# A hybrid decoder layer in float32: the 256 columns of the gate and up products walked in seven other orders

## The chip, the core and the metric

The kernel runs on one core of one Trainium2 chip, the other cores idle. The metric is device time in microseconds of one execution. It was timed twice: 2033.79 and 2034.99 us, median 2034.39. One more execution was taken by the hardware profiler; all lines of "the profile" and "the trace" come from it.

## The reference, cut to what matters

One decoder layer on 512 tokens plus 16 learned meta tokens, width 2048, all in float32:

```python
n = rmsnorm(h, g_mix);  q, k, v, gb, gc, u = split(n @ w_in)
o_attn = stick_breaking_attention(rmsnorm(q), rmsnorm(k), v)      # 8 heads x 128
o_conv = gb * causal_dwconv3(gc * u)                              # 1024 channels
h = h + concat(rmsnorm(o_attn), rmsnorm(o_conv)) @ w_out
n2 = rmsnorm(h, g_ffn)
h = h + (silu(n2 @ w_gate) * (n2 @ w_up)) @ w_down                # 2048 -> 5632 -> 2048
return h[:, 16:]
```

The change is in `n2 @ w_gate` and `n2 @ w_up`.

## The kernel before, in words

Everything is held transposed: channels on the 128 partitions, tokens along the row. Each float32 operand is split into a high part `hi` of TensorE's one-pass format (float32r, four bytes a value) and the rest `lo`, and a product is three products: hi by hi, hi by lo, lo by hi. Weights are the stationary operand in tiles of 128x128 (128 partitions, 128 columns), activations the moving rows, and the sums stand in PSUM.

The gate and up projections are done in **pairs**: for each of the 44 blocks f of 128 channels of the feed-forward, the gate tile and the up tile together form a 2x2 block product over two halves of the input channels and two halves of the tokens. It is done with 7 block products in place of 8, Strassen's way in Winograd's form: sums and differences of blocks go in, and sums of the products come out. `pair_product` (line 756) issues the seven in the order of the blocks 0, 1, 2, 3, 4, 5, 6 (block 5 first in a pair marked `first`) into three PSUM banks named x, z and y, and has ScalarE and VectorE copy or combine a bank behind each product. `block_product` (line 740) is one of the seven: it takes the next split weight block from `next_w` (hi and lo, 8 tiles each) and issues 3 x 8 = 24 matmuls of 256 columns (half of the 512 tokens) on line 754, all into the same 256 columns of one bank. A pair is 7 x 24 = 168 matmuls.

The same two functions also do the convolution's projections before (three times three pairs of 260 columns, moving rows from the tiles nh, nl and blk) and the down projection behind (moving rows from the tiles first and ring; in its first four pairs each bank holds two products side by side, m = 2). In the gate and up stage the moving rows lie in seven tiles f0 to f6. `slots` lays each out as [128 partitions, 2 parts, 8, 256], contiguous, with its data from the fifth element of the tile on; `act_of` hands out one row of 256 columns.

What else goes on during a pair: SyncE's queue loads the next weight quarters (line 172, 512 KB each) into w_buf, VectorE forms their sums (lines 207 and 225), ScalarE and VectorE split them into s_buf (lines 188 and 189), up to three blocks ahead of their use; `gate` (line 1062) forms silu(gate) * up out of gu, VectorE's lines 1064 and 1068 among it, and `store_acts` sends the blocks of the down projection to DRAM over GpSimd's queue (line 1056). The entries of the plan `ents` name the pair that each weight block belongs to; `used[0]` counts the blocks used so far; `conv_pairs` is the number of pairs of the convolution, so that pair number i - conv_pairs is the block f of the feed-forward.

Two other stages that the text speaks of: lines 286 to 290 (`product_steps`) do the input projection, 264 or 512 columns a matmul out of nh and nl, and lines 860 to 862 (`wide_product`) the output projection, 512 columns out of oa and oc.

Of the kernel before, what the change touches and what calls it, by code (L numbers as in the profile page):

```python
# [33 lines left out]
def hybrid_layer(ctx: ExitStack, tc: tile.TileContext, xT, w_in, w_out, w_gu, w_down, vecs, out):  # L34
# [10 lines left out]
    ve, sc, gp, pe = nc.vector, nc.scalar, nc.gpsimd, nc.tensor  # L45

    def open_pool(name, bufs=1, **kw):
        return tc.alloc_tile_pool(name=name, bufs=bufs, reuse_waits="tile", **kw)
# [54 lines left out]
    loads, ents, pairs = [], [], []  # L103
# [38 lines left out]
    conv_pairs = len(pairs)  # L142
# [11 lines left out]
    quads, sums, split_w, used, loaded = {}, {}, [], [0], [0]  # L154
# [25 lines left out]
    def ahead(e):  # L180
        return 3 if e > sixth + 2 else 2
# [27 lines left out]
    def prepare():  # L209
        i, s = ents[len(split_w)]  # L210
        with tc.high_priority():
            if i == "raw":
                split_quad(quads[i, s][0], loads[s][1])
                done_with((i, s))
                return
            n, first = pairs[i]
            second = i == conv_pairs + 1
            b = {q: quads[i, q][0] for q in ("11", "12", "21", "22") if (i, q) in quads}

            def add_t3():  # L220
                add_quads(i, "t3", b["12"], b["22"], second)
                done_with((i, "12"))

            def add_last():
                ve.tensor_tensor(sums["t2"], sums["t2"], b["21"], ALU.add)  # L225
                done_with((i, "21"))

            if s == 0:
                split_quad(b["11"], n, second)
                add_quads(i, "t1", b["11"], b["12"], second)  # L230
                done_with((i, "11"))
            elif s == 1:
                split_quad(sums["t1"], n, second)
                add_quads(i, "t2", sums["t1"], b["22"], second)
                if not first and not second:
                    add_t3()
            elif s == 2:
                split_quad(sums["t2"], n, second)
                if first or second:
                    add_t3()  # L240
            elif s == 3:
                split_quad(b["22"], n)
                done_with((i, "22"))
            elif s == 4:
                split_quad(sums["t3"], n)
            elif s == 5:
                split_quad(b["21"], n)
                if not first:
                    add_last()
            else:  # L250
                if first:
                    add_last()
                split_quad(sums["t2"], n, i == conv_pairs)
# [3 lines left out]
    def next_w():  # L257
        i = used[0]
        used[0] += 1
        while len(split_w) < limit[0] and len(split_w) <= i + ahead(len(split_w)):  # L260
            prepare()
        return split_w[i]
# [423 lines left out]
    for j in range(CONV_FIRST):  # L686
# [4 lines left out]
        for c in (c1, c2):  # L691
            p = pp.tile([P, 2, 512], F32, tag="pp", name="pcu")
# [47 lines left out]
    def block_product(ps, act, start, m=1):  # L740

        hi, lo, n = next_w()
        w, n = ps.shape[-1] // m, n // m
        for wt, part in ((hi, 0), (hi, 1), (lo, 0)):
            for j in range(m):
                p, skip = ps[:, j * w : (j + 1) * w], m > 1 or not start  # L750
                for k in range(n):
                    kk = slice((j * n + k) * P, (j * n + k + 1) * P)
                    first = start and wt is hi and part == j == k == 0
                    pe.matmul(p, wt[:, kk], act(part, k), start=first, stop=wt is lo and k == n - 1, skip_group_check=skip)  # L754

    def pair_product(acts, c1, c2, sides, m=1, fourth=None, second=None):

# [17 lines left out]
        if first:  # L775
            block_product(y, acts[5], True, m)
        block_product(x, acts[0], True, m)
        with tc.high_priority(1 << 20):
            sc.copy(p1, x)
        block_product(z, acts[1], True, m)  # L780
        with tc.high_priority(1 << 20):
            sc.copy(p5, z)
# [140 lines left out]
    for i, j in enumerate(OUT_TILES):  # L923
        half, k = divmod(j, 8)
# [186 lines left out]
    first = open_pool("ring_first", side="right")  # L1111
# [147 lines left out]
```

## Time and profile before

| | |
|---|---|
| timed runs | 2033.79 and 2034.99 us, median 2034.39 |
| profiled execution, span from the first to the last instruction | 2030.6 us |
| the median less the span | 3.8 us |
| mean granted TensorE clock | 1.000 |
| TensorE busy | 2024.3 us, 16158 matmuls |
| VectorE, ScalarE, GpSimd busy | 1720.3, 1050.1, 381.1 us |
| matmuls of line 754 out of f | 7392, from 769.1 to 1607.5 us |
| DMA | 361.70 MB, mean 178 GB/s |

The profile gives no time of its own for the profiled execution, only its span; what lies around the span is taken from the median. How to read the lines: engines are PE (TensorE's matmuls), PEld (its weight loads, which overlap), DVE (VectorE), ACT (ScalarE), POOL (GpSimd), SP (SyncE). `L754 PE MATMUL x<-f,s_buf 128*128 128x256 f32` is line 754 of the kernel: a matmul into tile x out of moving rows f and weights s_buf, 128 rows by 128 columns of the array, 256 columns streamed. Numbers of buffers are left out of tile names. In the view of one line of the program the durations are the least, the median and the greatest in ns, and then come the first and the last start in us. In the timeline, like instructions that follow one another are merged: start, length, instruction, count. The modelled end of a matmul lies behind the start of the next, since they are pipelined; the distance of starts is what adds up to time.

### The profile page before, as it was taken

How to read it: one execution, taken by the hardware profiler on the slowest of the kernel's cores; microseconds unless marked ns; L12 is line 12 of the kernel's file. 1: busy time of each engine (PE TensorE's matmuls, PEld its weight loads, DVE VectorE, ACT ScalarE, POOL GpSimd, SP SyncE). 2: the span in 40 equal slices, each digit the busy share in tenths (PEclk: the TensorE clock that was granted, in tenths of full speed). 3: DMA queues.
4: the chain of work that ended last, by engine and by line, in shares of the span. 5: the costliest groups of instructions: out<-in, count | busy, mean ns of one | idle time of the engine just before them, and what ended most of it. 6: DMA issues, size and time to landing. Idle time of an engine off the chain costs nothing.

```text
span 2030.6 us, 39733 instructions
## 1 busy us (share of the span) xinstructions
PE 2024.3 (100%) x16158; PEld 1961.7 (97%) x16158; DVE 1720.3 (85%) x2202; ACT 1050.1 (52%) x1517; POOL 381.1 (19%) x532
## 2 busy tenths in 40 slices
PE   9999999999999999999999999999999999999999
PEld 8999999999998889999999999999999999999999
DVE  8788877588976779989989989989989989888887
ACT  7666666444444435555555555555555544444443
POOL 0111111220015440111110110110110252222111
PEclk9999999999999999999999999999999999999999
DMA  6243344753366557555555555555555999989864
GB/s 232 84 147 117 123 135 137 252 154 106 105 213 183 186 174 238 169 161 172 166 161 152 166 161 152 166 161 153 166 161 152 292 327 287 245 234 271 226 149 89
DMA packets 162279, 361.70 MB, mean 178 GB/s; under 512 B 13616, under 2 KB 74032, under 8 KB 162096
## 3 DMA queue, kind: packets, MB, share of 16 engines
q1 hardware_dynamic: 79744, 229.47, 35.4%
q0 software_dynamic: 82208, 129.65, 24.4%
q8 instruction: 127, 2.08, 0.4%
q14 instruction: 56, 0.46, 0.1%
q10 hardware_dynamic: 144, 0.04, 0.0%
HBM read 278.50 MB, written 80.61 MB: 177 GB/s over the span
## 4 chain that ended last, share of the span: by engine, by line
PE 97%; DVE 1%; ACT 1%; issue 0%; DMA 0%; POOL 0%; SPq 0%; DVEq 0%; ACTq 0%
PE x L754 40%; PE z L754 20%; PE y L754 10%; PE po L860 3%; PE po L861 3%; PE po L862 3%; PE pv L286 1%; PE pv L288 1%; PE pv L290 1%; PE pq L288 1%; PE pq L290 1%; PE pq L286 1%; PE pk L286 1%; PE pk L288 1%; PE pk L290 1%; PE pcu L286 1%
## 5 line engine op out<-in xcount | busy, mean ns | idle before, releaser
L188 ACT CAST s_buf<-w_buf 128x1024 fp32r<-128x1024 f32 (+2 forms) x665 | 659.3, 991 | 747.7 <-PE x L754 370.7
L189 DVE TENSOR_TENSOR s_buf<-w_buf,s_buf 128x1024 fp32r<-128x1024 f32 (+2 forms) x665 | 766.5, 1153 | 121.2 <-ACT s_buf L188 119.1
L754 PE MATMUL x<-f,s_buf 128*128 128x256 f32 x4224 | 500.4, 275 | 0.0
L754 PEld LDWEIGHTS x<-f,s_buf 128*128 128x128 f32 x4224 | 488.8, 188 | 0.2
L207 DVE TENSOR_TENSOR w_buf<-w_buf 128x1024 f32<-128x1024 f32 (+1 forms) x243 | 278.3, 1145 | 18.5 <-DMA w_buf<-w_in 11.8
L754 PE MATMUL z<-f,s_buf 128*128 128x256 f32 x2112 | 253.6, 275 | 0.0
L754 PEld LDWEIGHTS z<-f,s_buf 128*128 128x128 f32 x2112 | 245.9, 188 | 0.0
L1056 POOL DMA_DIRECT2D fd<-s x147 | 103.9, 919 | 701.9 <-DVE s L301 701.1
L754 PE MATMUL x<-ring,s_buf 128*128 128x256 f32 x1824 | 219.2, 275 | 0.0
L754 PEld LDWEIGHTS x<-ring,s_buf 128*128 128x128 f32 x1824 | 212.5, 188 | 0.0
L754 PE MATMUL y<-f,s_buf 128*128 128x256 f32 x1056 | 126.8, 275 | 0.0
L754 PEld LDWEIGHTS y<-f,s_buf 128*128 128x128 f32 x1056 | 123.1, 188 | 0.1
L1129 POOL DMA_DIRECT2D out_T<-d x62 | 60.8, 1012 | 284.5 <-DVE d L1137 231.8
L754 PE MATMUL z<-ring,s_buf 128*128 128x256 f32 x864 | 105.7, 275 | 0.0
L754 PEld LDWEIGHTS z<-ring,s_buf 128*128 128x128 f32 x864 | 101.5, 188 | 0.0
L225 DVE TENSOR_TENSOR w_buf<-w_buf 128x1024 f32<-128x1024 f32 (+1 forms) x81 | 92.2, 1139 | 0.0
L754 PE MATMUL x<-nh,s_buf 128*128 128x260 f32 x432 | 58.9, 282 | 0.0
L790 DVE SCALAR_TENSOR_TENSOR gu<-z,sides 128x256 f32<-128x256 f32 x44 | 18.7, 425 | 42.7 <-PE z L754 40.8
L754 PEld LDWEIGHTS x<-nh,s_buf 128*128 128x128 f32 x432 | 54.5, 188 | 0.1
L754 PE MATMUL z<-blk,s_buf 128*128 128x260 f32 x432 | 54.6, 282 | 0.0
L286 PE MATMUL pk<-nh,s_buf 128*128 128x264 f32 x256 | 52.6, 287 | 0.5 <-ACT nh L358 0.5
L754 PEld LDWEIGHTS z<-blk,s_buf 128*128 128x128 f32 x432 | 52.9, 188 | 0.0
(344 smaller groups left out, 3318.3 us busy)
## 6 DMA issues: line engine op xcount, KB each, us to landing
w_buf<-w_gu SPq DMA_DIRECT2D x176, 512.0 KB, 3.5
w_buf<-w_in SPq DMA_DIRECT2D x92, 512.0 KB, 3.4
fd<-s POOLq DMA_DIRECT2D x147, 256.0 KB, 5.3
w_buf<-w_down SPq DMA_DIRECT2D x96, 384.0 KB, 4.9
ring<-fd POOLq DMA_DIRECT2D x42, 768.0 KB, 9.0
w_buf<-w_out SPq DMA_DIRECT2D x32, 512.0 KB, 3.5
out_T<-d POOLq DMA_DIRECT2D x62, 256.0 KB, 5.6
fc<-st SPq DMA_DIRECT2D x8, 1040.0 KB, 6.3
```

The source lines that it names most:

```text
L188: sc.copy(hi, src)
L189: in_turn(ve.tensor_tensor(lo, src, hi.bitcast(F32), ALU.subtract), turn)
L207: in_turn(ve.tensor_tensor(sums[name], a, b, ALU.add), turn)
L225: ve.tensor_tensor(sums["t2"], sums["t2"], b["21"], ALU.add)
L286: pe.matmul(ps, wh, ah[:, a:b], start=k == 0, stop=False)
L288: pe.matmul(ps, wh, al[:, a:b], start=False, stop=False)
L290: pe.matmul(ps, wl, ah[:, a:b], start=False, stop=k == last)
L754: pe.matmul(p, wt[:, kk], act(part, k), start=first, stop=wt is lo and k == n - 1, skip_group_check=skip)
L860: pe.matmul(ps, hi[:, kk], ah, start=k == order[0], stop=False)
L861: pe.matmul(ps, hi[:, kk], al, start=False, stop=False)
L862: pe.matmul(ps, lo[:, kk], ah, start=False, stop=k == order[-1])
L1056: gp.dma_start(fd[c][s][:, :, k], t[:, :, i])
```

## The change

`block_product` looks up which pair it serves, and in pairs 4 to 31 of the 44 gate and up pairs hands the matmul both its result and its moving row through `walk`. That views the 256 columns as h bands of b runs of e neighbouring columns and goes through them run by run, the first run of each band, then the second of each, and so on. The same order is used on both sides, so each column's sum ends where it did. With (h, e) = (2, 2), for instance, the columns come as 0, 1, 128, 129, 2, 3, 130, 131 and so on; with (2, 64) as 0 to 63, 128 to 191, 64 to 127, 192 to 255. Pairs 0 to 3 and 32 to 43, the convolution and the down projection keep their plain order. Seven groups of four pairs have a walk each: pairs 4 to 7 (2, 2); 8 to 11 (2, 4); 12 to 15 (2, 16); 16 to 19 (2, 64); 20 to 23 (4, 16); 24 to 27 (4, 4); 28 to 31 (8, 16).

```diff
+        i = ents[used[0]][0]
         hi, lo, n = next_w()
         w, n = ps.shape[-1] // m, n // m
         for wt, part in ((hi, 0), (hi, 1), (lo, 0)):
...
-                    pe.matmul(p, wt[:, kk], act(part, k), start=first, stop=wt is lo and k == n - 1, skip_group_check=skip)
+                    pe.matmul(walk(p, i), wt[:, kk], walk(act(part, k), i), start=first, stop=wt is lo and k == n - 1, skip_group_check=skip)
+
+    WALKS = {1: (2, 2), 2: (2, 4), 3: (2, 16), 4: (2, 64), 5: (4, 16), 6: (4, 4), 7: (8, 16)}
+
+    def walk(t, i):
+
+        g = WALKS.get((i - conv_pairs) // 4) if conv_pairs <= i < conv_pairs + 32 else None
+        if g is None:
+            return t
+        return t.rearrange("p (h b e) -> p b h e", h=g[0], e=g[1])
```

## The prediction

> **What bounds the kernel now.** I read the page first, then the stretch of the changed pairs in the table by stage, then the matmul rows of the line that is edited, and last single stretches of the timeline to get the pitch (start of one matmul to start of the next) of each kind of matmul.
>
> ```profile
> span 2030.6 us, 39733 instructions
> PE 2024.3 (100%) x16158; PEld 1961.7 (97%) x16158; DVE 1720.3 (85%) x2202; ACT 1050.1 (52%) x1517; POOL 381.1 (19%) x532
> PEclk9999999999999999999999999999999999999999
> PE 97%; DVE 1%; ACT 1%; issue 0%; DMA 0%; POOL 0%; SPq 0%; DVEq 0%; ACTq 0%
> ```
>
> TensorE is busy from end to end at an undiminished clock, and 97% of the chain that ended last is its own matmuls. So time added to a matmul is added to the kernel one for one, and time saved on one is saved until another engine takes over. The next two rows are the first four of the 28 changed pairs (846.2 to 922.4 us) and the twelve unchanged ones behind the last changed one; the columns behind the length of the stretch are busy time of PE, of its weight loads, of DVE, ACT and POOL, then the granted clock, the DMA share and GB/s.
>
> ```profile
> 846.20:922.40 76.20, 76.20 (x674) 76.20 (x674) 68.57 (x77) 39.32 (x53) 11.35 (x16) 1.00 0.60 174
> 1379.40:1607.50 228.10, 228.10 (x2015) 228.10 (x2014) 205.31 (x229) 117.15 (x157) 36.88 (x52) 1.00 0.59 172
> ```
>
> TensorE has no gap in a group; the nearest other engine, DVE, has 68.57 us of work in 76.20, so it would become the bound only if the matmuls got over 10% faster. Now the edited line itself:
>
> ```profile
> L754 PE MATMUL x<-f,s_buf x4224: 275/275/386, 771.9 to 1607.5; 128*128 128x256 f32 x192
> L754 PE MATMUL z<-f,s_buf x2112: 275/275/275, 774.6 to 1599.4; 128*128 128x256 f32 x192
> L754 PE MATMUL y<-f,s_buf x1056: 275/275/282, 769.1 to 1604.8; 128*128 128x256 f32 x176
> ```
>
> The 275 ns is the length of one with its fill and drain; they overlap. The number that matters is the pitch: 4224 + 2112 + 1056 = 7392 matmuls start between 769.1 and 1607.5 us, so (1607.5 - 769.1) / 7392 = 0.1134 us, **113.4 ns** for 256 columns. Three more places say what this pitch is made of. The timeline of a changed pair, then of a convolution pair (260 columns), then of the output projection (512 columns); columns are start, length of the merged run, instruction, count:
>
> ```profile
> 848.75 2.88 PE L754 MATMUL z<-f,s_buf 128*128 128x256 f32 x24
> 851.47 2.88 PE L754 MATMUL x<-f,s_buf 128*128 128x256 f32 x24
> 854.19 2.88 PE L754 MATMUL z<-f,s_buf 128*128 128x256 f32 x24
> ```
>
> ```profile
> 500.10 3.04 PE L754 MATMUL x<-blk,s_buf 128*128 128x260 f32 x24
> 502.98 3.04 PE L754 MATMUL z<-blk,s_buf 128*128 128x260 f32 x24
> ...
> 505.85 1.11 PE L754 MATMUL x<-nh,s_buf 128*128 128x260 f32 x8
> 506.80 1.11 PE L754 MATMUL x<-nl,s_buf 128*128 128x260 f32 x8
> ```
>
> ```profile
> 682.11 0.39 PE L860 MATMUL po<-oa,s_buf 128*128 128x512 f32 x1
> ...
> 686.87 0.39 PE L860 MATMUL po<-oa,s_buf 128*128 128x512 f32 x1
> ```
>
> In the changed pairs (851.47 - 848.75) / 24 = 113.3 ns, or 0.443 ns a column. In the output projection 21 matmuls lie between the two starts: 4.76 / 21 = 226.7 ns, again 0.443 ns a column. Twice the columns cost exactly twice, so nothing fixed is left in a matmul: the streaming of the columns is the whole bound. And the convolution pairs, with the same line and the same number of weight loads, take (502.98 - 500.10) / 24 = 120.0 ns from blk and 0.95 / 8 = 118.8 ns from nh, 0.462 and 0.457 ns a column, 3 to 4% more for rows that only lie elsewhere in SBUF. So **where** the moving rows lie already changes the pitch. A stream that had speed in hand would swallow such hitches; this one doesn't, so it runs at the edge of what delivers its data.
>
> **The change part by part.** Pairs 0 to 3 and 32 to 43 keep their access patterns, as do the convolution and the down projection. In pairs 4 to 31 every matmul gets the same columns in another order, moving rows and result alike. Instructions, weight loads, bytes, waits and sums stay: a group is 4 pairs x 7 products x 24 matmuls = 672 matmuls, 28 pairs are 4704. No DMA, no semaphore and no other engine's operand is touched, so the only term is 4704 times a change of pitch.
>
> What a walk does, with h bands, runs of e neighbouring columns and a jump after each run: group 1 (2, 2) has 128 runs of 2 columns (8 bytes) a matmul, group 2 (2, 4) 64 runs of 4, group 3 (2, 16) 16 of 16, group 4 (2, 64) 4 of 64, group 5 (4, 16) 16 of 16, group 6 (4, 4) 64 of 4, group 7 (8, 16) 16 of 16. No matmul in this trace walks a broken row, so each price has to be bounded.
>
> The nearest row with a jump in it is on VectorE: line 1068 writes two runs of 256 columns with a gap of 256 between, line 1064 the same 512 columns unbroken.
>
> ```profile
> L1064 DVE TENSOR_TENSOR gu<-gu,acc_h x44: 682/684/693, 797.5 to 1609.5; 128x512 f32<-128x512 f32 x44
> L1068 DVE TENSOR_TENSOR even<-gu,gu x22: 685/686/693, 800.3 to 1593.0; 128x512 f32<-128x512 f32 x22
> ```
>
> 686 against 684 ns: a single long jump costs nothing there worth the name. That is the lower bound, **0** for every group (below nothing: see the fourth rival). The upper bound for a walk is that each visit to a place delivers only half as much, as if 512 columns were streamed: 226.7 ns, a loss of 113.4 ns a matmul, 672 x 113.4 = **76.2 us a group**.
>
> Between these ends I go by the length of the run. Every unbroken row here starts and ends on a multiple of four columns (rows start at 4, 8, 16 and at steps of 256 or 260), so no row shows what happens to a piece below four. For runs of 4, 16 and 64 (groups 2 to 7) I take 0, the end at which the VectorE row lies: each visit still brings a whole multiple of what all rows here are cut in. For runs of 2 (group 1) I take the upper end, because the stream has no speed in hand: if the port fetches pieces of four columns, as I assume, each is fetched twice, and 128 half-used fetches take the time of 128 whole ones, which is the 512-column pitch. That the smallest whole piece is four and not two is a judgement, and it is the weak step of the sum.
>
> [...]
>
> The sum: the execution profiled has a span of 2030.6 us; the two timed runs have a median of 2034.4, so 3.8 us lie around the span and stay. Group 1 +76.2, groups 2 to 7 0: span 2106.8, time 2034.4 + 76.2 = **2110.6 us** (+3.7%). What is late next: in group 1 the weights' casts and differences, the gates and the DMAs get twice the time for the same work (DVE 68.57 us in about 152), so they only wait longer for TensorE and nothing new ends up behind them.
>
> **The rivals.**
>
> *All walks are free* (the other side: not slower). What the port fetches at a time would be no more than two columns, or both bands' pieces would be held until their other half is asked for. For it: result and rows keep pairs of neighbours in every group, and the single jump on VectorE cost nothing. Against it: the pitch answers to the place of the rows, which a port with such room would hide. It decides where the price of group 1 falls under 40.7 us / 672 = 61 ns a matmul. Time: 2034 us, give or take the fourth rival's shift.
>
> *Runs of four pay too.* Groups 1, 2 and 6 jump after every piece or half piece, and by 64 or 128 columns (256 or 512 bytes), so to places that agree in their low address bits; if the memory behind is laid out in banks by those bits, successive fetches hit one bank. For it: the convolution rows, whose pitch goes with address alone. Against: those hitches are 3 to 4%, not 100%. At the upper bound three groups pay: 3 x 76.2 = 228.6, time 2263 us.
>
> *Any broken row is slow.* If the streaming unit or the result's side only keeps its rate on unbroken rows, all seven groups pay: 7 x 76.2 = 533 us, time 2568. For it: not one matmul of this kernel is broken, so the trace can't exclude it. Against: runs of 64 columns give it 64 orderly steps for each jump. [...]
>
> *The walks move the hitches.* A new order of places can remove or add as much as place does between the rows above: 120.0 ns for 260 columns against 0.443 x 260 = 115.1, so up to 4.9 ns either way, 4704 x 4.9 = 23 us: 2011 to 2057. All of the gain at once needs every group to be lucky. It also is the error bar on the forecast. DVE's 68.57 us in 72.9 would still be cover.
>
> *A price for each jump.* If a jump costs one column's time (0.443 ns), the runs add 128 + 64 + 16 + 4 + 16 + 64 + 16 = 308 per matmul of each group: 308 x 672 x 0.443 ns = 92 us, time 2126, spread over the groups by their runs instead of in the first alone.
>
> **How the numbers follow.** Forecast 0.40; all free 0.25; runs of four pay too 0.15; any broken row 0.08; only shifted hitches with a gain 0.05; a price for each jump 0.07. The time is that of the likeliest, 2110.6. Its own range is 2072 (group 1 at half price) to 2134 (all hitches against it). The range to hold 8 in 10 goes from 2025, which takes in the free case with a small shift, to 2268, which takes in the three-group case; left out are the 0.08 above and most of the 0.05 below, and half-cases beyond. A measurement of this kernel can tell about 2% (40.7 us) from no change. Slower by over 2%: 0.40 + 0.15 + 0.08 + 0.07, less a little for group 1 at a half price: 0.68. Within 2%: 0.25 + 0.05 and that little: 0.31. Faster by over 2% would need 8.7 ns off each of 4704 matmuls, more than place has been seen to do: 0.01.
>
> **What would show it right or wrong.** The three matmul rows of the edited line still count 4224, 2112 and 1056. The timeline's pitch by group decides: right is about 226 ns in pairs 4 to 7 (a product of 24 every 5.44 us instead of 2.72, the group 152 us long) and 113 to 118 ns in pairs 8 to 31. The free case shows 2.72 us everywhere; the bank case 5 us in groups 1, 2 and 6; the broken-row case 5 us in all seven, with 2.72 again from pair 32 on; the price by jumps a staircase, 170, 142, 120 and 115 ns for 128, 64, 16 and 4 runs. The convolution, output and down stages must keep their lengths; if one of them grew, the cause would lie outside the walks and the prediction would be wrong in kind. It is wrong in its main step if group 1 keeps its pitch or if any group with runs of 16 takes over 130 ns.

## The result and the profile after

The changed kernel takes 2104.62 us (median of 2 runs, 2103.98 to 2105.27) against 2034.39: ratio 1.0349, 95% interval 1.0319 to 1.0379. It is 70.2 us slower; forecast were 76.2. The page of the changed kernel, the lines that answer to those shown of before:

```profile
span 2103.6 us, 39761 instructions
PE 2094.7 (100%) x16158; PEld 2032.1 (97%) x16158; DVE 1724.3 (82%) x2202; ACT 1053.6 (50%) x1517; POOL 380.4 (18%) x532
PE 96%; DVE 2%; ACT 1%; DMA 1%; issue 0%; POOL 0%; SPq 0%; DVEq 0%; ACTq 0%
```

TensorE has the same 16158 matmuls and is still 96% of the chain, at a granted clock of 1.000; its busy time grew with the span. Where it grew is read from the table by stage, cut at the starts of the seven groups. The columns are stretch, length, busy time of PE, of its weight loads, DVE, ACT and POOL, clock, DMA share, GB/s; the last row is the twelve unchanged pairs behind.

```profile
848.70:961.40 112.70, 112.70 (x675) 112.70 (x674) 70.01 (x77) 40.60 (x53) 11.31 (x16) 1.00 0.39 118
961.40:1046.50 85.10, 85.10 (x674) 85.10 (x673) 69.42 (x76) 39.78 (x52) 9.87 (x14) 1.00 0.49 143
1046.50:1127.10 80.60, 80.60 (x674) 80.60 (x673) 68.52 (x76) 39.37 (x53) 9.88 (x14) 1.00 0.52 150
1127.10:1203.40 76.30, 76.30 (x675) 76.30 (x674) 68.52 (x77) 39.28 (x53) 9.83 (x14) 1.00 0.55 159
1203.40:1281.80 78.40, 78.40 (x675) 78.40 (x674) 68.99 (x77) 39.17 (x53) 9.88 (x14) 1.00 0.53 156
1281.80:1372.30 90.50, 90.50 (x675) 90.50 (x674) 69.79 (x77) 41.17 (x53) 9.85 (x14) 1.00 0.45 135
1372.30:1452.00 79.70, 79.70 (x673) 79.70 (x673) 68.74 (x76) 39.29 (x53) 9.88 (x14) 1.00 0.52 153
1452.00:1680.50 228.50, 228.50 (x2018) 228.50 (x2017) 205.37 (x229) 117.69 (x157) 36.87 (x52) 1.00 0.59 171
```

A group is 672 matmuls (a row also counts the two or three that reach into it), so length / 672 is the pitch, to 0.15 ns; and length less the 76.2 us of before is what the group costs.

| pairs | walk (bands, run) | length, us | pitch, ns | added, us |
|---|---|---|---|---|
| 4 to 7 | (2, 2) | 112.7 | 167.7 | 36.5 |
| 8 to 11 | (2, 4) | 85.1 | 126.6 | 8.9 |
| 12 to 15 | (2, 16) | 80.6 | 119.9 | 4.4 |
| 16 to 19 | (2, 64) | 76.3 | 113.5 | 0.1 |
| 20 to 23 | (4, 16) | 78.4 | 116.7 | 2.2 |
| 24 to 27 | (4, 4) | 90.5 | 134.7 | 14.3 |
| 28 to 31 | (8, 16) | 79.7 | 118.6 | 3.5 |

The seven add up to 69.9 us, nearly all of what the kernel lost. Nothing took the place of TensorE: DVE has some 69 us of work in every group. The twelve pairs behind keep their 228 us, and the down projection its 419. (The two profiled spans, 2030.6 and 2103.6 us, differ by 73.0 us. Of the 3.1 us that the seven groups leave, 2.7 came ahead of the change: the gate and up stage began at 771.8 us instead of 769.1. In the later runs it began between 767.8 and 769.4. Why it was late in this one execution is not known.)

So the total came within 8% of the forecast, but nearly half of it is where it was not put: group 1 pays half of its 76.2 us, and the six groups that were put at nothing pay 33.4 together.

### The profile page after: what moved, and what is told of

Read it like the earlier page. It is cut to its first block, busy times and chain, and to the rows that moved or that the text cites. A ratio compares the mean times of both kernels' runs of the same rounds, so it can differ in the third digit from the quotient of the medians.

```text
span 2103.6 us, 39761 instructions
## 1 busy us (share of the span) xinstructions
PE 2094.7 (100%) x16158; PEld 2032.1 (97%) x16158; DVE 1724.3 (82%) x2202; ACT 1053.6 (50%) x1517; POOL 380.4 (18%) x532
## 4 chain that ended last, share of the span: by engine, by line
PE 96%; DVE 2%; ACT 1%; DMA 1%; issue 0%; POOL 0%; SPq 0%; DVEq 0%; ACTq 0%
PE x L755 41%; PE z L755 20%; PE y L755 10%; PE po L872 3%; PE po L870 3%; PE po L871 3%; PE pv L286 1%; PE pv L288 1%; PE pv L290 1%; PE pk L286 1%; PE pk L290 1%; PE pk L288 1%; PE pq L288 1%; PE pq L290 1%; PE pq L286 1%; PE pcu L286 1%
## 5 line engine op out<-in xcount | busy, mean ns | idle before, releaser
L755 PE MATMUL x<-f,s_buf 128*128 128x256 f32 x4224 | 540.9, 286 | 0.0
L755 PEld LDWEIGHTS x<-f,s_buf 128*128 128x128 f32 x4224 | 528.0, 189 | 0.2
L755 PE MATMUL z<-f,s_buf 128*128 128x256 f32 x2112 | 273.8, 286 | 0.0
L755 PEld LDWEIGHTS z<-f,s_buf 128*128 128x128 f32 x2112 | 265.3, 189 | 0.0
L755 PE MATMUL y<-f,s_buf 128*128 128x256 f32 x1056 | 137.0, 286 | 0.0
L755 PEld LDWEIGHTS y<-f,s_buf 128*128 128x128 f32 x1056 | 132.7, 189 | 0.1
L286 PE MATMUL pv<-nh,s_buf 128*128 128x264 f32 x256 | 52.9, 287 | 0.0
```

The lines of the kernel that those rows point to most:

```text
L286: pe.matmul(ps, wh, ah[:, a:b], start=k == 0, stop=False)
L755: pe.matmul(walk(p, i), wt[:, kk], walk(act(part, k), i), start=first, stop=wt is lo and k == n - 1, skip_group_check=skip)
```

## The experiments

Each kernel gives every group of four pairs its own setting, so that one profile is a table of pitches; the groups are numbered from 1 (pairs 4 to 7) to 10 (pairs 40 to 43), and pairs 0 to 3 stay plain. What was to be told apart: whether the price arises where the rows are read or where the result is added; if it is the rows, whether it is their fetches in lines of four columns, each jump, or a collision with the weight loads. A line stands in what follows for four neighbouring columns that begin at a multiple of four; it is a way to count, and no run shows a fetch. In the later kernels a group's setting is written as (walk of the rows, walk of the result, columns that the row begins later, columns that the weight tile begins later). All rows below are of the table by stage, one for each group named. Each of these kernels but the last was run once, so a group is compared with groups of plain rows in the same or another run: those took 76.1 or 76.2 us a group every time, 113.2 to 113.4 ns.

### One side alone: rows_only and result_only

```diff
-                    pe.matmul(walk(p, i), wt[:, kk], walk(act(part, k), i), start=first, ...
+                    pe.matmul(p, wt[:, kk], walk(act(part, k), i), start=first, ...            # rows_only
+                    pe.matmul(walk(p, i), wt[:, kk], act(part, k), start=first, ...            # result_only
```

> Only the moving rows are walked in the seven orders; the result is written in plain order, so in pairs 4 to 31 each sum lands in another token's column. Theory R (the price arises where the moving rows are read): the seven groups keep the pitches of the changed kernel, 167.6, 126.7, 120.0, 113.4, 116.7, 134.7, 118.7 ns, and the time stays near 2105 us. Theory P (it arises where the result is added in PSUM): all groups at 113.3 ns and near 2034 us. A mixture would show each group between.

> Only the result is walked; the moving rows are read in plain order, so in pairs 4 to 31 each sum lands in another token's column. Theory R: all seven groups at 113.3 ns, near 2034 us. Theory P: the pitches of the changed kernel, near 2105 us. If the two sides each pay and the slower decides, the larger of this run and of the run with walked rows is the changed kernel's pitch, group by group.

Walked rows, groups 1 and 6, 2103.8 us in all beside 2032.9 of the kernel before on that chip:

```profile
846.20:958.90 112.70, 112.70 (x675) 112.70 (x674) 70.02 (x77) 40.65 (x53) 11.33 (x16) 1.00 0.39 118
...
1279.30:1369.80 90.50, 90.50 (x675) 90.50 (x674) 69.80 (x77) 41.10 (x53) 9.88 (x14) 1.00 0.45 135
```

Walked result, the same groups, 2033.1 us in all:

```profile
845.90:922.00 76.10, 76.10 (x674) 76.10 (x673) 68.43 (x77) 39.20 (x53) 11.32 (x16) 1.00 0.59 173
...
1226.70:1302.80 76.10, 76.10 (x674) 76.10 (x673) 68.45 (x77) 39.20 (x53) 9.86 (x14) 1.00 0.53 159
```

As clear as it can be: with the rows walked every group has the changed kernel's length to 0.1 us, with the result walked every group has the old one. The price is one of reading the moving rows. Seven broken patterns into PSUM, down to runs of two, cost nothing: 113.2 to 113.4 ns a matmul. (Runs of one on the result's side weren't tried.)

### Lines of four, or jumps: pieces and odd_pieces

```diff
+        1: ((4, 2), (4, 2), 0, 0),          # pieces
...
+        5: ((64, 2), (64, 2), 0, 0),
...
+        8: ((16, 4), (16, 4), 0, 0),
...
+        1: ((2, 1), None, 0, 0),            # odd_pieces
+        2: ((64, 1), None, 0, 0),
...
+        5: ((2, 4), None, 2, 0),
+        6: ((2, 4), None, 4, 0),
```

> Ten other walks on both sides, outputs as the reference's: (4,2), (8,2), (16,2), (32,2), (64,2), (32,4), (8,4), (16,4), (2,8), (2,32). Theory L (rows are fetched in pieces of four columns; a piece visited twice is fetched twice, and a fetch takes 1.31 ns at the most often, 128 of them 167.6 ns): the first five all near 167.6 ns, those with runs of 4 to 32 between 113 and 135, with no order by the number of jumps. Theory J (a price for each jump of 0.2 to 0.42 ns): 128 jumps 139 to 167, 64 jumps 126 to 140, 32 jumps (2, 8) 120 to 127, 8 jumps (2, 32) 115 to 117, in that order. Under a theory of jump distance (64, 2), whose jumps are of four columns, would be far cheaper than (4, 2).

> Only the moving rows are walked, so sums land in other columns. Groups 1 to 4: runs of a single column, (2,1), (64,1), (128,1), (32,1); groups 5 and 6: (2,4) begun 2 and 4 columns later, so that each run of group 5 lies across two pieces of four and each of group 6 in one; group 7: (2,16) begun 2 later; groups 8 to 10: (4,8), (16,8), (8,8). Theory L (pieces of four columns, 1.31 ns each when they bound): groups 1 to 4 make 256 fetches, 335 ns; group 5 makes 128, near 167 ns, against 127 to 135 in group 6; group 7 makes 80, near 120 to 125. Theory J (a price for each jump, 0.2 to 0.42 ns, wherever the run lies): groups 1 to 4 113.3 + 256 x 0.42 = 221 ns at most, group 5 as group 6.

From pieces, groups 1 (4, 2), 5 (64, 2), 7 (8, 4) and 8 (16, 4):

```profile
845.00:997.30 152.30, 152.30 (x674) 139.53 (x673) 70.33 (x77) 41.27 (x53) 11.31 (x16) 1.00 0.30 90
...
1456.10:1608.40 152.30, 152.30 (x673) 139.55 (x672) 69.91 (x76) 40.72 (x52) 9.88 (x14) 1.00 0.26 79
...
1687.60:1768.30 80.70, 80.70 (x675) 80.70 (x674) 68.92 (x77) 39.60 (x53) 9.88 (x14) 1.00 0.50 151
1768.30:1844.40 76.10, 76.10 (x674) 76.10 (x673) 68.24 (x77) 39.12 (x53) 9.89 (x14) 1.00 0.53 158
```

152.3 / 672 = 226.6 ns, twice the plain pitch: the other three walks with runs of 2 take 222.6, 233.3 and 226.8, so all five are dearer than either theory had them (167.6 at the most). Runs of 4 take 120.1 in (8, 4), 117.9 in (32, 4) and 113.2 in (16, 4), with 64 jumps a matmul. So it is not the number of jumps: 64 of them can be free, and (2, 8) with 32 jumps costs what (2, 4) costs with 64, 126.8 against 126.6 ns. For half-used lines a count of lines fits: a plain row visits 64 lines of four columns at 113.3 / 64 = 1.77 ns each, a walk with runs of 2 visits 128, half used, at the same 1.77 (226.6 / 128). That (64, 2), whose jumps are of four columns only, costs the same as (4, 2) with its 64 says that distance is not it either. The forecast's full price for half-used lines, 226.7 ns, is right for every number of bands but two.

From odd_pieces, groups 1 (2, 1), 2 (64, 1), 5 and 6 (the runs of 4 across two lines, and in one):

```profile
845.50:920.60 75.10, 75.10 (x675) 75.10 (x675) 68.33 (x77) 39.60 (x53) 11.32 (x16) 1.00 0.59 176
920.60:1077.40 156.80, 156.80 (x675) 139.78 (x674) 70.32 (x77) 41.00 (x53) 9.88 (x14) 1.00 0.26 81
...
1377.50:1491.30 113.80, 113.80 (x674) 113.79 (x674) 69.60 (x76) 40.11 (x52) 9.88 (x14) 1.00 0.34 104
1491.30:1578.60 87.30, 87.30 (x673) 87.30 (x673) 69.42 (x76) 40.49 (x52) 9.86 (x14) 1.00 0.46 139
```

Groups 5 and 6 differ only by where (2, 4) begins: 169.3 ns when each run lies across two lines, 129.9 when it lies in one. A plain row begun at these two places takes 121.0 and 120.1 ns (late_rows below), so the place as such is worth 1 ns. So it counts whether a run lies in one line of four or across two, and that is worth 39 ns here. What a visit costs is less settled: (2, 16) begun 2 columns later visits 80 lines, 80 x 1.77 = 141.7, measured 143.2; but begun in place, with 64 visits, it takes 119.9 and not 113.3, so the agreement is in part luck, and (2, 4) across lines makes 128 visits and takes 169.3 in place of 226.7. And both theories fall on runs of one. (64, 1) touches a new line with every column, 256 visits, and takes 233.3 ns like the 128 visits above, neither 335 nor 221; (128, 1) and (32, 1) take 228.9 and 217.7. And (2, 1), 128 columns this way and that with every single column, takes 75.1 / 672 = **111.8 ns, less than the plain row**.

This led to theory T, a guess at what could lie behind these pitches: columns would be taken two at a time, the first and the second of each pair by a taker of its own that keeps the line it has. In (64, 1) a pair would need two new lines, but at once, so 128 steps, as with runs of 2 (233.3 ns beside 222.6 to 233.3); in (2, 1), 111.8 ns, each taker would run through a band of its own and get all four columns of a line before it needs the next.

### The takers, and the place: readers

```diff
+        1: ((4, 1), None, 0, 0),
+        2: ((8, 1), None, 0, 0),
...
+        6: ((2, 1), None, 16, 0),
...
+        9: ((2, 1), None, 0, 16),
```

> Only the moving rows are walked, so sums land in other columns; groups 1 to 3 are (4,1), (8,1), (16,1) in place; groups 4 to 8 are (2,1), measured at 111.7 ns in place, with the row begun 4, 8, 16, 32, 48 columns later; groups 9 and 10 are (2,1) with the weight tiles begun 16 and 32 columns later. Theory T (columns are taken in pairs, the first and the second of each pair by a taker of its own that keeps the four-column line it fetched last; a line costs 1.77 ns): in (2,1) each taker runs through its own unbroken row, so it is cheap; (4,1) sends each taker to and fro between two lines as (2,2) did, near 167 ns; (8,1) and (16,1) between four and eight, 218 to 233 ns. Theory E (runs of one column are simply read another way when bands are far apart): (4,1), (8,1), (16,1) near 112. On place: if a taker with four columns a line has speed in hand, (2,1) stays within 1 ns of 111.7 in groups 4 to 10; if not, 113 to 120.

Groups 1, 2, 6 and 9:

```profile
846.30:940.40 94.10, 94.10 (x675) 94.10 (x674) 69.94 (x77) 40.28 (x53) 11.31 (x16) 1.00 0.47 141
940.40:1089.70 149.30, 149.30 (x674) 139.09 (x673) 69.94 (x76) 41.07 (x53) 9.88 (x14) 1.00 0.27 84
...
1387.60:1462.70 75.10, 75.10 (x675) 75.10 (x675) 68.39 (x77) 39.36 (x53) 9.86 (x14) 1.00 0.54 163
...
1612.80:1687.80 75.00, 75.00 (x674) 75.00 (x673) 68.24 (x77) 39.46 (x53) 9.87 (x14) 1.00 0.54 163
```

(8, 1) takes 222.2 ns and (16, 1) 219.9, as theory T has it and against theory E. (4, 1), where by theory T each taker would go to and fro between two lines, takes 140.0: dearer than plain, but below the 167 that were expected. Like (2, 2) with its 167.7 ns it is cheaper than the five walks with runs of 2 and more bands, 222.6 to 233.3; by what means is open. And (2, 1) takes 111.6 to 111.8 ns in all seven groups, wherever rows or weights begin. By theory T it would have speed in hand, since each taker would use four columns of every line; that is a reading of the pitches, and no run shows the takers themselves.

All walks of a row in its old place, with full weights, pitch in ns (a plain row takes 113.3):

| | 2 bands | 4 | 8 | 16 | 32 | 64 | 128 |
|---|---|---|---|---|---|---|---|
| runs of 1 | 111.8 | 140.0 | 222.2 | 219.9 | 217.7 | 233.3 | 228.9 |
| runs of 2 | 167.7 | 226.6 | 226.8 | 222.6 | 233.3 | 226.6 | plain |
| runs of 4 | 126.6 | 134.7 | 120.1 | 113.2 | 117.9 | plain | |
| runs of 8 | 126.8 | 127.8 | 115.6 | 117.3 | plain | | |
| runs of 16 | 119.9 | 116.7 | 118.6 | plain | | | |
| runs of 32 | 119.9 | | | | | | |
| runs of 64 | 113.5 | | | | | | |

Where it says "plain", bands of one run each leave the row as it was.

### The place of a plain row: late_rows, places

```diff
+            at = (part * 8 + k) * T2 + (late if part * 8 + k < 15 else 0)        # the row begins `late` columns later
...
+                    if wt_late and k < n - 1:        # the weight tile too (places)
+                        kk = slice(kk.start + wt_late, kk.stop + wt_late)
```

> No walk at all: in pairs 4 to 43 the plain moving row of 256 columns begins 1, 2, 4, 8, 12, 16, 24, 32, 36 or 48 columns later than it should (one number for each group of four pairs; the last of the 16 rows of a tile is left where it is), so the sums are of shifted columns. Theory R1 (the port fetches pieces of four columns and only whole pieces matter): the shifts by 1 and 2 cost up to one more piece in 64, 113.3 to 116 ns, and every multiple of four stays at 113.3. Theory R2 (the fetches of the moving row run into those of the weights at certain places): the pitch differs among the multiples of four too, as between the places of the convolution's rows, some 113 to 121 ns, or below 113.3 at a lucky place; whole run 2025 to 2060 us.

> No walk; four pairs a group as before. Groups 1 to 4 begin the weight tiles 4, 16, 32, 60 columns later (rows unmoved), groups 5 to 8 begin rows and weights both later by 4, 16, 32, 48 columns, groups 9 and 10 begin the rows alone 20 and 60 columns later; the last tile or row of a block is left where it is, and the sums are of shifted data. Theory W (what counts is the row's place relative to the weights read beside it): groups 5 to 8 return to 113.3 ns, groups 1 to 4 rise to 117 to 120. Theory M (the row's own place counts): groups 1 to 4 stay at 113.3, and groups 5 to 8 show the 120.0, 118.9, 117.2 and 118.3 ns that rows alone showed at these shifts.

From late_rows, begun 1, 4 and 16 columns later; then from places, the weights alone 4 later, and rows and weights both 4 later:

```profile
846.20:928.80 82.60, 82.60 (x674) 82.60 (x673) 69.18 (x77) 39.59 (x53) 11.34 (x16) 1.00 0.55 160
...
1010.10:1090.80 80.70, 80.70 (x675) 80.70 (x674) 68.67 (x77) 39.52 (x53) 9.89 (x14) 1.00 0.51 150
...
1250.50:1330.40 79.90, 79.90 (x675) 79.90 (x674) 68.93 (x77) 39.45 (x53) 9.87 (x14) 1.00 0.50 152
```

```profile
844.70:925.40 80.70, 80.70 (x675) 80.70 (x674) 69.17 (x77) 39.59 (x53) 11.32 (x16) 1.00 0.55 165
...
1164.50:1244.20 79.70, 79.70 (x675) 79.70 (x674) 68.82 (x77) 39.26 (x53) 9.88 (x14) 1.00 0.51 152
```

A plain row begun 1 later takes 122.9 ns, 2 later 121.0, 4 later 120.1, 16 later 118.9; the other multiples of four 117.3 to 119.5, and 20 later, in places, 115.6. R1 falls. The 113.3 ns of the kernel before are the pitch of a favoured place. Moving the weights alone, by 4, 16, 32 or 60, also ends it (120.1, 118.3, 117.4, 120.1 ns), so the weight loads take part: theory M falls. But moving both by the same does not bring it back (118.6, 117.7, 117.7, 119.5): W as I put it falls too. (Where weights are moved, the last of each eight tiles stays where it was, and of 16 rows the last, which blurs this one.)

### Narrow weights: narrow and narrow_plain

```diff
+                    last = wt is lo and k == n - 1
+                    c = P if first or last or not conv_pairs + 4 <= i < conv_pairs + 32 else 32        # narrow
+                    pe.matmul(walk(p, i)[:c], wt[:, kk][:, :c], walk(act(part, k), i), start=first, ...
```

> The seven walks on both sides as in the changed kernel, but 22 of the 24 matmuls of a block product in pairs 4 to 31 use only 32 of the 128 weight columns, so their weight loads read a quarter and three quarters of the sums are left out. Theory R1 (the price is the moving row's own fetches): the pitches stay at 167.6, 126.7, 120.0, 113.4, 116.7, 134.7, 118.7 ns. Theory R2 (the moving row runs into the weight loads): the prices shrink to about a quarter, for instance group 1 near 127 ns and group 6 near 119, and the plain order comes below 113.3 ns, towards 108.

> 22 of 24 matmuls use 32 weight columns in place of 128, so three quarters of the sums are left out; groups 1 to 5 are plain rows begun 0, 4, 16, 32, 48 columns later (113.3, 120.0, 118.9, 117.2, 118.3 ns with full weights), 6 and 7 the rows walked (2,1) begun 0 and 16 later, 8 (4,2), 9 (4,4), 10 (2,16). [...]

From narrow, groups 1 (2, 2), 3 (2, 16), 5 (4, 16) and 6 (4, 4); from narrow_plain, the plain row begun 4 later, (2, 1) in place, and (4, 2):

```profile
845.00:955.50 110.50, 110.50 (x675) 79.66 (x673) 69.92 (x77) 40.35 (x53) 11.32 (x16) 1.00 0.40 120
...
1038.90:1119.50 80.60, 80.60 (x674) 73.06 (x673) 68.51 (x77) 39.41 (x53) 9.87 (x14) 1.00 0.51 150
...
1196.10:1274.60 78.50, 78.50 (x675) 73.13 (x674) 68.99 (x77) 39.19 (x53) 9.87 (x14) 1.00 0.52 156
1274.60:1364.30 89.70, 89.70 (x675) 75.32 (x673) 69.77 (x77) 40.80 (x53) 9.86 (x14) 1.00 0.45 136
```

```profile
921.70:998.60 76.90, 76.90 (x674) 72.87 (x673) 68.51 (x77) 39.18 (x53) 9.88 (x14) 1.00 0.53 158
...
1230.80:1304.20 73.40, 73.40 (x674) 73.30 (x673) 67.71 (x77) 39.23 (x53) 9.85 (x14) 1.00 0.54 164
...
1377.70:1527.80 150.10, 150.10 (x674) 88.20 (x673) 70.50 (x77) 41.26 (x53) 9.89 (x14) 1.00 0.28 85
```

This parts two things. With a quarter of the weights to read in 22 of 24 matmuls (a load of 32 columns shows 110 ns in the profile of narrow, one of 128 columns 188), the walks keep most of their prices: group 1 at 164.4 ns, (2, 4) at 124.1, (2, 16) at 119.9, (4, 16) at 116.8, group 6 at 133.5 and (4, 2) at 223.4; only (8, 16) gives back half of its price or more, 115.9. Theory R2 falls for the walks: group 1 was to come near 127 ns and group 6 near 119. But the plain rows at other places come down from between 117 and 120 ns to 114.3 and 114.4 (begun 4, 32 and 48 later; 117.0 at 16), so most of what a place costs a plain row goes with the weights. (Narrow weights also write only 32 of the 128 rows of the result, so this run alone doesn't say that it is the loads; places does, where the weight tiles alone were moved and the result was not.) The plain row in its favoured place doesn't fall, 114.0 ns, and the 108 that theory R2 gave it, an estimate of the author's, is shown by no run; (2, 1) falls to 109.2. So the 1.5 ns between these two in the kernels with full weights do not go with the weights: with narrow ones they are 4.8.

### The same walks at another place: walks_late; other distances: distances

```diff
+        3: ((2, 16), (2, 16), 16, 0),       # walks_late
...
+        8: (None, None, 16, 0),
+        9: ((2, 16), (2, 16), 32, 0),
...
+            two_bands = flat[:, at : at + 2 * d].rearrange("p (h d) -> p h d", h=2)[:, :, :128]     # distances: bands d columns apart
```

> The seven walks again on both sides, but with the moving rows of groups 1 to 7 begun 16 columns later, where a plain row was measured at 118.9 ns; group 8 is the plain row at that place, groups 9 and 10 are the walks (2, 16) and (2, 4) begun 32 columns later, where plain was 117.2; the sums are of shifted columns. Theory A (a walk with runs of 16 costs only because it loses the good place that the plain row has): groups 3, 5 and 7 come within 2 ns of the plain 118.9, and group 9 within 2 of 117.2. Theory B (each jump has its price, whatever the place): they come to 118.9 + 6.7, + 3.3 and + 5.3, that is 125.6, 122.2, 124.2 ns, and group 9 to 123.9. Group 1 stays near 168 to 173 by either.

> Only the moving rows are changed: two bands of 128 columns, walked by turns in runs of 4 (groups 1 to 7, whole lines), 16 (group 8) or 2 (groups 9 and 10), where the second band begins D columns behind the first, D = 128, 132, 136, 144, 160, 192, 256, then 144, then 132 and 160; for D over 128 some columns come from the next row and some are left out, so the sums are of other data. Theory B (lines that agree in low address bits hinder each other when fetched one behind the other; 128 columns are 512 bytes): group 1 repeats 126.7 ns, groups 2 to 6 fall to 113 to 118, group 7 returns to 127 to 135; group 8 falls from 120.0 to 113 to 117. Theory J (the jump itself costs, however far): groups 1 to 7 all near 126.7, group 8 at 120. Groups 9 and 10: 167.6 if only the half use of a line counts; if group 1 of the change was cheaper than the 226.7 ns of other half-used lines because its two bands agree in their low bits, they come to 226.7.

From walks_late, groups 3 (2, 16), 5 (4, 16), 7 (8, 16) and 8 (plain):

```profile
1047.10:1127.90 80.80, 80.80 (x674) 80.80 (x674) 68.55 (x76) 39.42 (x53) 9.90 (x14) 1.00 0.50 150
...
1207.80:1289.40 81.60, 81.60 (x674) 81.60 (x673) 68.87 (x77) 39.46 (x53) 9.90 (x14) 1.00 0.50 149
...
1380.50:1459.70 79.20, 79.20 (x674) 79.20 (x673) 68.64 (x76) 39.29 (x53) 9.90 (x14) 1.00 0.51 153
1459.70:1539.60 79.90, 79.90 (x674) 79.90 (x673) 68.99 (x77) 39.46 (x53) 9.91 (x14) 1.00 0.50 152
```

Against a plain 118.9 ns at the new place the three walks with runs of 16 stand at 120.2, 121.4 and 117.9: their price is 1.3, 2.5 and -1.0 ns in place of 6.6, 3.4 and 5.3. (2, 16) begun 32 later takes 120.4 against a plain 117.3. Theory B falls for groups 3 and 7, but theory A, that such a walk costs only the plain row's favoured place, missed its own 2 ns in two of four, and the narrow weights speak against it: they free most of what a plain row pays elsewhere, and (2, 16) in place stays at 119.9, (4, 16) at 116.8. What the pitches show is that a walk's price and a place's price do not add up: (2, 16) takes 119.9 to 120.4 ns at all three places and with either width of weights. Why is open. Groups 1, 2 and 6 stay dear (171.3, 128.1, 135.6).

From distances, two bands in runs of 4, 128, 144 and 192 columns apart, and in runs of 2, 132 apart:

```profile
845.10:930.20 85.10, 85.10 (x674) 85.10 (x673) 69.70 (x77) 40.06 (x53) 11.34 (x16) 1.00 0.53 156
...
1100.10:1181.70 81.60, 81.60 (x675) 81.60 (x674) 68.84 (x77) 40.22 (x53) 9.85 (x14) 1.00 0.49 150
...
1264.40:1349.50 85.10, 85.10 (x675) 85.10 (x674) 69.41 (x77) 39.98 (x53) 9.87 (x14) 1.00 0.48 143
...
1515.40:1626.10 110.70, 110.70 (x674) 110.70 (x673) 69.74 (x77) 40.36 (x53) 9.88 (x14) 1.00 0.36 110
```

126.6 ns at 128, 121.4 at 144, 126.6 again at 192 (256: 126.6; 132: 128.7; 136: 124.1; 160: 123.1); runs of 16 at 144 stay at 120.2. Theory B, that only places alike in their low address bits hinder one another, falls: no distance brings the pitch back to 113 to 118. Theory J is nearer for two bands, but (16, 4), with as many jumps, costs nothing. And (2, 2) is no dearer at 132 and 160 columns (164.7, 163.1), so its discount against 226.7 does not come from a distance of just 512 bytes. (The last of 16 rows stays plain in this kernel, one matmul in 24.)

### A version that is faster than both: apart

If (2, 1) is cheaper than a plain row, store the rows so that this walk hands out the natural order: the even tokens of each half first, then the odd ones. The splits that write f0 to f6 and the blocks for the down projection read their source with a step of two; the result isn't walked at all.

```diff
+    def split_apart(hi, lo, src, turn=False):          # in split_f, the stages for DRAM, store_acts
...
+            src = src.rearrange("p (b h) -> p h b", h=2)
...
-                    pe.matmul(p, wt[:, kk], act(part, k), start=first, ...
+                    row = act(part, k)
+                    row = row.rearrange("p (h b) -> p b h", h=2) if apart else row
+                    pe.matmul(p, wt[:, kk], row, start=first, ...
```

> The kernel before with one new idea: the activations of the gate, up and down products are stored with the even tokens of a half in front of the odd ones, and the moving rows are walked (2,1), which hands the columns to TensorE in their natural order; results are written in plain order. Theory T: all 11088 matmuls of these stages take 111.7 in place of 113.3 ns, 18.5 us less, 2016 us, ratio 0.991. Rival: reading every second column in the splits of ScalarE and VectorE or the new places of the rows give it back, ratio 1.00.

Measured: 2016.00 us (median of 5, 2015.71 to 2017.42) against 2031.95 of the kernel before on the same chip, ratio **0.9923**, interval 0.9910 to 0.9937. The table by stage, gate and up and then down; then ScalarE's casts in the splits, in this kernel and in the kernel before (durations least, median, greatest in ns):

```profile
769.00:1595.50 826.50, 826.14 (x7394) 825.67 (x7393) 758.25 (x849) 451.41 (x581) 116.62 (x165) 1.00 0.56 169
1595.60:2010.10 414.50, 413.15 (x3698) 412.77 (x3696) 360.36 (x491) 196.69 (x281) 99.95 (x119) 1.00 0.88 240
```

```profile
L300 ACT CAST s<-odd x22: 1658/1675/1692, 816.7 to 1603.5; 128x1280 fp32r<-128x1280 f32 x22
```

```profile
L300 ACT CAST s<-odd x22: 1270/1271/1275, 816.9 to 1614.4; 128x1280 fp32r<-128x1280 f32 x22
```

The gate and up stage shrank by 12 us (838.4 to 826.8, from its own first matmul), the down projection by 4 (418.9 to 414.5, with 1.4 us of idle time in it): 16 us, somewhat less than the 18.5 that were expected. Its ten groups of four pairs take 75.0 or 75.1 us, so the pitch of (2, 1), 111.6 to 111.8 ns, holds where the walk hands out the natural order; whether takers are behind it this run doesn't say. ScalarE pays for the step of two, 1675 ns in place of 1271 for five blocks, and that lies beside the matmuls: it is busy 451 us of 826.

## Why the prediction was right, and where it was wrong

**Bound and sign.** Right, for the reason given: the stream of moving rows is the whole bound, it answers to order (111.6 to 233.3 ns) and place (113.3 to 122.9 ns for a plain row), and what the matmuls lose the kernel loses: 69.9 us in the seven groups, 70.2 in all. Not every broken row loses: (2, 64) and (16, 4) run plain, 113.5 and 113.2 ns, and (2, 1) gains, 111.8. The result's side, which the prediction left in doubt, is free (113.2 to 113.4 ns).

**Group 1 at the upper end.** The direction was right and the size off. That a port fetches pieces of four columns was the author's assumption, and no run shows a fetch. In its place the runs show pitches: (2, 4) takes 169.3 ns with its runs across two lines of four and 129.9 with each in one, and the 226.7 ns of the forecast are what all five walks from (4, 2) to (64, 2) take to within 7. The walk in question, with two bands, takes 167.7, by the prediction's own sign ("about 226 ns") a miss: 36.5 us in place of 76.2. That two bands are cheaper than four or more was not foreseen, and why they are is open.

**Runs of 4 and 16 at nothing.** This is the step that failed, for 33.4 us. "Each visit still brings a whole multiple of what all rows here are cut in" is true, and it did not make the visits free: whole lines in some orders are dearer than in their own, by 0 ns for (16, 4), 7 for (8, 4), 13 for (2, 4) and (2, 8), 21 for (4, 4). Most of this is the walk's own. Groups 2 and 6 (8.9 and 14.3 us) keep it at another place and with narrow weights; so do (2, 16) and (4, 16) with narrow weights, 119.9 and 116.8 ns beside a plain 114.0. Only (8, 16) comes down with them as a plain row out of its place does. Neither the number of jumps nor the distance orders these prices; the cause is open. There was a warning in the rows: the prediction had seen the convolution's rows at 118.8 and 120.0 ns and used them as an error bar of either sign. The changed pairs stood at the low end of all rows shown, and ten of ten other places of a plain row at multiples of four proved dearer (115.6 to 120.1), so the bar should have been drawn longer on the side of a loss.

**The rivals.** The price for each jump came nearest in shape: its staircase of 170, 142, 120 and 115 ns stands beside 167.7, 126.6 to 134.7, 116.7 to 119.9 and 113.5. Yet it is not the mechanism: 64 jumps cost nothing in (16, 4), 128 cost twice as much in (4, 2) as in (2, 2), and 255 make (2, 1) faster. That runs of four pay too was half right, at 12 to 19% of the price it set. Broken rows as such are not slow: (2, 64) and (16, 4), at 113.5 and 113.2 ns, are free. All walks free fell with group 1 (167.7 ns), though its 36.5 us alone stay under the 40.7 us at which the prediction drew the line between the two.

**Where the two errors met.** 40 us too much in group 1 and 33 too little in the others nearly cancel. That the total came so near is luck, and so is the clear slowdown: group 1 alone would have given 1.8%, inside the 2% that the prediction called no change. Only the pitch by group could show it.

## What to carry to other kernels

Where TensorE's pitch scales with the columns alone (here 113.3 ns for 256, 226.7 for 512), compare the pitch per column of the same instruction over all stages. Here it differed with nothing but the place of the rows, 0.443 beside 0.457 and 0.462 ns, and a change of order or place moved it; the best row shown had more to lose than to gain, 2.3 to 6.8 ns at ten other places against 1.6 gained by the best walk. For moving rows of four bytes a column, the walks with runs of 2, half of a line of four columns at a visit, took 167.7 ns with two bands, half as much again as a plain row, and 222.6 to 233.3 with more, about twice as much. Walks of whole lines, with the row in its old place, took from 113.2 ns, as a plain row does, to 134.7, 19% dearer, so measure the order that is meant. The order of the result in PSUM was free in all seven walks that were tried on it alone, 113.2 to 113.4 ns. And a sum that fits isn't yet a mechanism that fits: split the change by group, and each side of it by itself.

## What was not expected of the hardware

Reading two bands of a row by turns, one column from each, was faster than reading the row straight: 111.7 against 113.3 ns for 256 columns, and the same at all places of rows and weights that were tried, where the straight row took from 113.3 to 120.1 at multiples of four. With narrow weights it took 109.2 ns beside the straight row's 114.0. ScalarE's cast of 1280 elements took 1675 ns with a step of two elements against 1271 without.
